# Reading moving operands and writing product columns in descending order in two stages of a two-layer decoder trunk

## The chip, the core and the metric

The kernel runs on one core of one Trainium2 chip. The metric is the device time of one execution in microseconds (us). Before the change it is 2561.69 us, the median of three runs (2560.36 to 2563.14 us). A profile of one execution gives the times of single instructions; its span, from the first to the last instruction, is 2558.4 us.

## The reference, cut to what matters

The reference is a decoder trunk on 256 tokens of width 2048, with two layers, in float32. Each layer has a token mixer (layer 0: multi-scale retention; layer 1: a short gated convolution) and a SwiGLU feed-forward of inner width 5632. Each of the four sublayers starts with an RMS norm that is scaled and shifted by columns computed from a conditioning vector.

```python
for i in range(DEPTH):
    mod = (c_act @ w_mod[i] + b_mod[i])[:, None, :]
    sh1, sc1, g1, sh2, sc2, g2 = jnp.split(mod, 6, axis=-1)
    h = rms_norm(x, norm1_g[i]) * (1.0 + sc1) + sh1
    y = retention_mixer(...) if i == 0 else short_conv_mixer(...)
    x = x + g1 * y
    h = rms_norm(x, norm2_g[i]) * (1.0 + sc2) + sh2
    x = x + g2 * swiglu(h, ffn_w_in[i], ffn_w_out[i])

def swiglu(h, w_in, w_out):
    a, b = jnp.split(h @ w_in, 2, axis=-1)
    return (jax.nn.silu(a) * b) @ w_out

def short_conv_mixer(h, w_in, conv_w, w_out):
    b_gate, c_gate, u = jnp.split(h @ w_in, 3, axis=-1)
    u = c_gate * u
    up = jnp.pad(u, ((0, 0), (CONV_WIDTH - 1, 0), (0, 0)))
    y = sum(conv_w[j] * up[:, j:j + S] for j in range(CONV_WIDTH))
    return (b_gate * y) @ w_out
```

The products that the change touches are `h @ w_in` of layer 0's feed-forward, and `h @ w_in` and `(...) @ w_out` of the convolution mixer in layer 1.

## The kernel before, in words

Every float32 factor is split into a high part (type fp32r) and a low remainder, fp32r as well. A product is then high times high, plus high times low, plus low times high. All matmuls contract over 128 partitions. The weights come from HBM in tiles of 128x2048 (`raw`, issued by `fetch`, L380), in exactly the order of use; `prepare` splits each into `hi` (ScalarE, L419) and `lo` (VectorE, L422), which lie in two rings of five places of 1024 columns. Five places ahead of the matmuls is as far as the splitting can run. VectorE also computes the conditioning columns (`modulation`, L326) between the other work.

There are two main forms of product.

- `product` (L472 and L475): a block of 128x128 weights is the stationary operand, and the activation rows are the moving one. A row tile holds the high part of 256 tokens and beside it the low part, so that one matmul of 512 columns (L472) multiplies the weights' high part by both, into a whole PSUM bank of two halves, and one of 256 columns (L475) multiplies the weights' low part by the high rows alone, into the bank's second half. Both matmuls load their stationary operand anew. One block of weights thus costs a pair of matmuls. The two halves are added when the bank is read (`summed`, or the two L714 and L715 operations of `output`).
- `thrice` (L485, L486, L487): a 128x128 piece of activations is the stationary operand, and 512 columns of weights are the moving one. The three matmuls, all of 512 columns, are high times high, high times low, low times high, into one bank.

Layer 0's feed-forward is done in two parts of 20 and 24 column tiles. `first_rows` makes the last four tiles of the first part with `normed` and `product`. All others come from `last_input`, ten times in all: `gathered` runs over eight pairs of row tiles, where five pairs go through `by_token` (eight calls of `thrice` each) and three through `sevens` (seven calls of `thrice` in place of eight, with sums of activation pieces as the stationary operands, in tiles named `sums` and `u`). That is 61 calls of `thrice` for each `last_input`, 610 in all. At the end of `last_input`, eight transposes (L1290), which wait in a list and are run inside the next group, turn the result for the second matrix. The second matrix of layer 0's feed-forward goes through `output` and `product`.

The convolution in layer 1 has 48 column tiles of its first matrix: five in `normed` (L667 to L669), 43 in `product` (43 x 16 = 688 pairs). Its second matrix has 15 tiles in `product` (240 pairs), and the last in `packed`.

Layer 1's feed-forward uses `thrice` for both matrices, with the same code as layer 0's first matrix. The retention has both forms.

The order of the matmuls is that of the program (the matrix engine's schedule is written by hand); the other engines' order is the planner's. The weights' layout in HBM follows the order of use and is checked at each `take`. The dictionary `own` holds what differs between the callers of `gathered`.

Of the kernel before, what the change touches and what calls it, by code (L numbers as in the profile page):

```python
# [44 lines left out]
FFN_TILES, FFN_SEVEN, FFN_TURNS = (20, 24), (2, 4, 6), 2  # L45
# [219 lines left out]
def trunk(ctx: ExitStack, tc: tile.TileContext, x_in, c_in, pos_in, w_mod, cols_in, gain_in, tab_in, w_all, out):  # L265
# [8 lines left out]
    def name(s):  # L274
        serial[0] += 1
        return f"{s}_{serial[0]}"

    def tmp(tag, shape=(P, S), dtype=F32, pool=work, bufs=None):
        return pool.tile(list(shape), dtype, tag=tag, name=name(tag), bufs=bufs)
# [69 lines left out]
    def paced(n):  # L349

        units[0] += n
        due = 0
        for (a, i), (b, j) in zip(plan_mod, plan_mod[1:]):
            if units[0] >= a:
                due = min(j, i + (units[0] - a) * (j - i) // (b - a))
        allowed[0] = min(allowed[0] + n * MOST, 2.0)
        while todo and n_mod - len(todo) < due and allowed[0] >= 1.0:
            allowed[0] -= 1.0
            modulation(*todo.pop())
# [71 lines left out]
    def fits():  # L431
        return prepared[0] < len(pieces) and len(ready) + 1 + (pieces[prepared[0]][1] == 6) <= PLACES

    def take(group, k, col, width=P):

        assert order.pop() == (group, k, col, width)
        i = place[0] or 0
        if i == 0:
            if place[0] == 0:
                ready.pop(0)  # L440
            while len(ready) < 1 + AHEAD * (units[0] >= first) or units[0] >= early and fits():
                n = len(ready)
                prepare()
                if len(ready) == n:
                    break
        place[0] = (i + width) % ready[0][2]
        return [t[:, i : i + width] for t in ready[0][:2]]

    def bank():
        return ps.tile([P, 2, S], F32, tag="bank", name=name("bank"))  # L450

    asides, since = [], [0]
    waiting = []

    def ticked(n):

        since[0] += n
        if asides and since[0] >= asides[0][0]:
            asides.pop(0)[1]()
            since[0] = 0  # L460

    def product(g, act, base=0, before=None, banks=None, last=True):

        fresh = not banks
        banks = banks or [bank() for _ in g.cols]
        for k in g.ks:
            if before:
                before(k)
            h = act[k - base]
            for c, pt in zip(g.cols, banks):  # L470
                hi, lo = take(g, k, c)
                nc.tensor.matmul(  # L472
                    pt, hi, h, start=fresh and k == g.ks[0], stop=False, skip_group_check=True
                )
                nc.tensor.matmul(  # L475
                    pt[:, 1, :], lo, h[:, 0, :], start=False, stop=last and k == g.ks[-1], skip_group_check=True
                )
            ticked(len(g.cols))
            paced(len(g.cols))
        return banks  # L480

    def thrice(o, x, w, first, last):

        (hi, lo), (w_hi, w_lo) = x, w
        nc.tensor.matmul(o, hi, w_hi, start=first, stop=False)  # L485
        nc.tensor.matmul(o, hi, w_lo, start=False, stop=False)  # L486
        nc.tensor.matmul(o, lo, w_hi, start=False, stop=last)  # L487
# [140 lines left out]
    def rows_at(o):  # L628
        return [
            h_all[:, o + 2 * S * j : o + 2 * S * (j + 1)].rearrange("p (a b) -> p a b", a=2) for j in range(KT)  # L630
        ]

    h = rows_at(EARLIER)
# [88 lines left out]
    with ExitStack() as inner:  # L722
# [64 lines left out]
        with tc.tile_pool(name="start", bufs=1) as sp:  # L787
# [59 lines left out]
            with tc.manual_schedule(engines={mybir.EngineType.DVE, mybir.EngineType.Activation}):  # L847
# [10 lines left out]
                part = rm.tile([P, P], F32, tag="mid17", name="part")  # L858
# [24 lines left out]
                sums = bank()[:, 0, :]  # L883
# [52 lines left out]
                def before(k):  # L936
                    if k:
                        lows[k] = row(k)
# [210 lines left out]
        h = rows_at(0)  # L1149
# [9 lines left out]
        s = b()  # L1159
        nc.vector.tensor_tensor(m, s, g1, op=ALU.mult)  # L1160

    own = {}

    def at(v, c):
        return v[:, c * DV : (c + 1) * DV]

# [134 lines left out]
    def first_rows(firsts, pairs, layer, norm, turns=()):  # L1301

        pending, done = [], 0
        for i, g in enumerate(firsts):
            pending += [sums(g)] if i else normed(acc, layer, norm, g)
            while len(pending) >= 2:
                both = half_bank().rearrange("p (a b) -> p a b", a=2)
                g1, m = both[:, 0, :], both[:, 1, :]
                silu_times(*pending[:2], g1, m)
                pending = pending[2:]  # L1310
                split(pairs[done // 2][:, done % 2], m)
                done += 1
            for turn_of in turns[4 * (i - 1) : 4 * i] if i else ():
                turn_of()

    def paired(pool, n):

        return [pool.tile([P, 2, 2, S], F32R, tag=f"mid{i}", name=name("mid")) for i in range(n // 2)]

    with tc.tile_pool(name="ffn", bufs=1) as fpool:  # L1320
        h = rows_at(EARLIER)
        own.update(pool=fpool, sums={}, turns=FFN_TURNS)
        first_mid = paired(fpool, max(FFN_TILES))[: FFN_TILES[0] // 2]
        differences[0] = fpool.tile([P, 2 * DV], F32, tag="differences", name="differences")
        own["extra"] = [fpool.tile([P, DV], F32, tag=f"extra{i}", name=f"extra{i}") for i in range(2)]
        for part in range(2):
            n = FFN_TILES[part] // 2
            mid = paired(fpool, FFN_TILES[part]) if part else first_mid
            if not part:
                first_rows(FFN_FIRSTS, mid[-2:], 0, 1)  # L1330
                made_in_sums(FFN_SEVEN, [
                    fpool.tile([P, 2, P], F32R, tag=f"sums{i}", name=f"sums{i}") for i in range(6)
                ] + [tmp("u", (P, 2, P), F32R, bufs=3) for _ in range(3)])
            for i, groups in enumerate(FFN_IN[part]):
                last_input(groups, mid[2 * i : 2 * i + 2], [None, None])
            act = {k + part * FFN_TILES[0]: mid[k // 2][:, k % 2] for k in range(2 * n)}
            acc = output(
                FFN_OUT[part], act, (0, GT2), part == 1, (lambda j: scaled_only(1, 0, j)) if part else None, base=0
            )
        h = rows_at(0)  # L1340

    mixing = ctx.enter_context(ExitStack())
# [4 lines left out]
    for i, g in enumerate(CONV_IN):  # L1347
        pending += [sums(g)] if i else normed(acc, 1, 0, g)
        while len(pending) >= 3:
# [3 lines left out]
            b, c, u = pb(tmp("bsum", pool=mpool, bufs=2)), pc(), pu()  # L1353
# [13 lines left out]


    mixing.close()
    mpool = ctx.enter_context(tc.tile_pool(name="last", bufs=1))  # L1370
    dram = ctx.enter_context(tc.tile_pool(name="dram", bufs=1, space=bass.MemoryType.DRAM))

    mpool.tile([P, 120], F32, tag="apart", name="apart")
    h = rows_at(EARLIER)
# [34 lines left out]
    turns = [lambda t=t, c=c: turn(t, c) for c in range(4) for t in range(2)]  # L1409
# [149 lines left out]
```

## Time and profile before

| what | value |
|---|---|
| median of three runs | 2561.69 us (2560.36 to 2563.14) |
| profiled execution, first to last instruction | 2558.4 us |
| TensorE matmuls (PE) | 2539.3 us busy, 13237 instructions |
| TensorE weight loads (PEld) | 2181.4 us busy |
| VectorE (DVE) | 2354.7 us busy |
| ScalarE (ACT) | 1351.2 us busy |
| read from HBM | 685.11 MB, 269 GB/s over the span |

The profiled execution's own time is its span, 2558.4 us; the median of the runs lies 3.3 us above it, which is taken as what lies around the span. Matmuls are pipelined, and the end of each is modelled: a 512-column matmul is shown as 390 ns long while the next starts 227 ns after it. What counts for the time is the distance from one start to the next, called pitch below.

### The profile page before, as it was taken

To read this page: it belongs to the slowest core of one execution; us is meant where nothing else is said; L and a number is where in the kernel's file an instruction comes from. 1 tells how busy PE (TensorE), PEld (TensorE's weight loads), DVE (VectorE), ACT (ScalarE), POOL (GpSimd) and SP (SyncE) were. 2 spreads that over 40 slices of the span, in tenths; PEclk is the share of its full clock that TensorE was granted. 3 is DMA by queue.
4 is the path that set the end of the run, shared out by engine and by line. 5 is a ranking of instruction groups with operands and counts; after the bars stand their busy time and mean duration, and the time that the engine had idled before them with its cause. 6 is when DMAs were issued, how large, how long until landed. Compare 5 with 4: busy or idle time off the path is not lost.

```text
span 2558.4 us, 34761 instructions
## 1 busy us (share of the span) xinstructions
PE 2539.3 (99%) x13237; PEld 2181.4 (85%) x13237; DVE 2354.7 (92%) x2968; ACT 1351.2 (53%) x1799; POOL 179.3 (7%) x234
## 2 busy tenths in 40 slices
PE   8999999999999999999999999999999999999998
PEld 7898888888889888888888898888998888888886
DVE  7989999898899999889999899888989999999998
ACT  5544543454456554345555454445566555555554
POOL 0000121011110001000000012000000000000001
PEclk9999999999999999999999999999999999999999
DMA  9987888879875667866667879888846465555653
GB/s 399 396 329 264 319 317 340 333 287 331 325 281 213 237 234 293 336 249 228 216 228 299 328 270 344 314 306 309 323 158 215 180 230 214 181 214 183 228 183 146
DMA packets 96695, 689.47 MB, mean 269 GB/s; under 512 B 10744, under 2 KB 12168, under 8 KB 13456
## 3 DMA queue, kind: packets, MB, share of 16 engines
q1 hardware_dynamic: 96528, 687.25, 72.2%
q8 instruction: 103, 1.69, 0.3%
q14 instruction: 64, 0.52, 0.1%
HBM read 685.11 MB, written 2.11 MB: 269 GB/s over the span
## 4 chain that ended last, share of the span: by engine, by line
PE 94%; DVE 3%; DMA 1%; ACT 1%; issue 1%; POOL 0%; SPq 0%; ACTq 0%; POOLq 0%; DVEq 0%
PE bank L472 22%; PE bank L487 17%; PE bank L485 17%; PE bank L486 17%; PE bank L475 11%; DVE lo L422 1%; PE bank L667 1%; PE bank L669 1%; PE bank L668 1%; PE bank L536 1%; PE bank L535 1%; PE bank L534 1%; DVE raw L798 1%; DMA raw<-w_all 1%; PE bank L1290 1%; PE bank L1067 1%
## 5 line engine op out<-in xcount | busy, mean ns | idle before, releaser
L419 ACT CAST hi<-raw 128x1024 fp32r<-128x1024 f32 (+1 forms) x984 | 991.1, 1019 | 936.7 <-PE bank L487 325.1
L422 DVE TENSOR_TENSOR lo<-raw,hi 128x1024 fp32r<-128x1024 f32 (+1 forms) x984 | 1143.3, 1179 | 125.6 <-ACT hi L419 116.7
L485 PE MATMUL bank<-hi,h 128*128 128x512 f32 x1540 | 602.9, 391 | 0.0
L487 PE MATMUL bank<-hi,h 128*128 128x512 f32 x1540 | 601.2, 390 | 0.0
L486 PE MATMUL bank<-lo,h 128*128 128x512 f32 x1540 | 601.1, 390 | 0.0
L326 DVE SCALAR_TENSOR_TENSOR raw<-raw,cb 128x2048 f32<-128x2048 f32 x160 | 365.4, 2285 | 8.2 <-DMA raw<-w_mod 8.0
L472 PE MATMUL bank<-h,hi 128*128 128x512 f32 x1012 | 352.8, 392 | 0.0
L487 PEld LDWEIGHTS bank<-hi,h 128*128 128x128 f32 x1540 | 289.4, 188 | 61.0
L485 PEld LDWEIGHTS bank<-hi,h 128*128 128x128 f32 x1540 | 289.6, 188 | 58.1
L486 PEld LDWEIGHTS bank<-lo,h 128*128 128x128 f32 x1540 | 289.7, 188 | 57.5
L472 PE MATMUL bank<-mid,hi 128*128 128x512 f32 x920 | 319.4, 391 | 0.0
L475 PE MATMUL bank<-h,lo 128*128 128x256 f32 x1012 | 285.0, 282 | 0.0
L475 PE MATMUL bank<-mid,lo 128*128 128x256 f32 x920 | 259.7, 282 | 0.0
L472 PEld LDWEIGHTS bank<-h,hi 128*128 128x128 f32 x1012 | 190.1, 188 | 40.3
L472 PEld LDWEIGHTS bank<-mid,hi 128*128 128x128 f32 x920 | 172.9, 188 | 35.6
L475 PEld LDWEIGHTS bank<-h,lo 128*128 128x128 f32 x1012 | 191.6, 189 | 0.5
L475 PEld LDWEIGHTS bank<-mid,lo 128*128 128x128 f32 x920 | 174.3, 189 | 0.1
L472 PE MATMUL bank<-rm,hi 128*128 128x512 f32 x496 | 172.5, 391 | 0.0
L475 PE MATMUL bank<-rm,lo 128*128 128x256 f32 x496 | 140.0, 282 | 0.0
L487 PE MATMUL bank<-hi,mid 128*128 128x512 f32 x284 | 110.9, 391 | 0.0
L485 PE MATMUL bank<-hi,mid 128*128 128x512 f32 x284 | 110.9, 391 | 0.0
L486 PE MATMUL bank<-lo,mid 128*128 128x512 f32 x284 | 110.7, 390 | 0.0
(300 smaller groups left out, 3344.2 us busy)
## 6 DMA issues: line engine op xcount, KB each, us to landing
raw<-w_all SPq DMA_DIRECT2D x456, 1024.0 KB, 5.0
raw<-w_mod SPq DMA_DIRECT2D x192, 1024.0 KB, 6.1
x<-x_in SPq DMA_DIRECT2D x4, 512.0 KB, 5.3
out<-xt SPq DMA_DIRECT2D x4, 512.0 KB, 3.0
decay<-tab_in SPq DMA_DIRECT2D x8, 128.0 KB, 4.9
x<-gate_row SPq DMA_DIRECT2D x2, 512.0 KB, 4.6
last_gain<-gain_in SPq DMA_DIRECT2D x1, 1024.0 KB
cols<-cols_in SPq DMA_DIRECT2D x1, 152.0 KB, 8.2
```

What stands on the lines that cost most here:

```text
L326: nc.vector.scalar_tensor_tensor(raw, raw, 1.0, cb, op0=ALU.mult, op1=ALU.mult, accum_out=total)
L419: nc.scalar.copy(hi[:, o], raw[:, o])
L422: nc.vector.tensor_tensor(lo, raw, hi.bitcast(F32), op=ALU.subtract)
L472: nc.tensor.matmul(pt, hi, h, start=fresh and k == g.ks[0], stop=False, skip_group_check=True)
L475: nc.tensor.matmul(pt[:, 1, :], lo, h[:, 0, :], start=False, stop=last and k == g.ks[-1], skip_group_check=True)
L485: nc.tensor.matmul(o, hi, w_hi, start=first, stop=False)
L486: nc.tensor.matmul(o, hi, w_lo, start=False, stop=False)
L487: nc.tensor.matmul(o, lo, w_hi, start=False, stop=last)
L534: nc.tensor.matmul(pt, hi, h[:, 0, :], start=first, stop=False, skip_group_check=True)
L535: nc.tensor.matmul(pt, hi, h[:, 1, :], start=False, stop=False, skip_group_check=True)
L536: nc.tensor.matmul(pt, lo, h[:, 0, :], start=False, stop=last, skip_group_check=True)
L667: nc.tensor.matmul(pt, hi, high, start=k == 0, stop=False, skip_group_check=True)
```

## The change: direction of columns

Two switches are added, both off at first. With `downward`, `thrice` gives the matmul its moving operand (512 columns of weights) and its output (a PSUM bank) with the columns in descending order: step -1 in place of +1, from the last column to the first. With `rows_downward`, `product` does the same with the moving row tile (512 columns, or the 256 of its high half) and the bank. Each product lands in the same place as before, since operand and output are turned together. `downward` is on from the beginning of layer 0's feed-forward to its end, where only the first matrix uses `thrice`; `rows_downward` is on from there to the end of the convolution. The number and order of instructions, the addresses of all tiles, the transfers and the waits stay as they are.

```diff
+    own = {}
...
             for c, pt in zip(g.cols, banks):
                 hi, lo = take(g, k, c)
+                both, rows, end, high = pt, h, pt[:, 1, :], h[:, 0, :]
+                if own.get("rows_downward"):
+                    both, rows = [v.rearrange("p a b -> p (a b)")[:, ::-1] for v in (pt, h)]
+                    end, high = end[:, ::-1], high[:, ::-1]
                 nc.tensor.matmul(
-                    pt, hi, h, start=fresh and k == g.ks[0], stop=False, skip_group_check=True
+                    both, hi, rows, start=fresh and k == g.ks[0], stop=False, skip_group_check=True
                 )
                 nc.tensor.matmul(
-                    pt[:, 1, :], lo, h[:, 0, :], start=False, stop=last and k == g.ks[-1], skip_group_check=True
+                    end, lo, high, start=False, stop=last and k == g.ks[-1], skip_group_check=True
                 )
...
     def thrice(o, x, w, first, last):
 
         (hi, lo), (w_hi, w_lo) = x, w
+        if own.get("downward"):
+            o, w_hi, w_lo = [v[:, ::-1] for v in (o, w_hi, w_lo)]
         nc.tensor.matmul(o, hi, w_hi, start=first, stop=False)
...
-    own = {}
...
         h = rows_at(EARLIER)
-        own.update(pool=fpool, sums={}, turns=FFN_TURNS)
+        own.update(pool=fpool, sums={}, turns=FFN_TURNS, downward=True)
...
                 FFN_OUT[part], act, (0, GT2), part == 1, (lambda j: scaled_only(1, 0, j)) if part else None, base=0
             )
+            own.update(downward=not part, rows_downward=bool(part))
         h = rows_at(0)
...
     mixing.close()
+    own["rows_downward"] = False
```

## The prediction

> **What bounds the kernel now.** I read the page's busy times first, then the granted clock and the chain of work that ended last, then stretches of time, one for each stage, and last the starts of single matmuls.
>
> ```profile
> span 2558.4 us, 34761 instructions
> ...
> PE 2539.3 (99%) x13237; PEld 2181.4 (85%) x13237; DVE 2354.7 (92%) x2968; ACT 1351.2 (53%) x1799; POOL 179.3 (7%) x234
> ...
> PEclk9999999999999999999999999999999999999999
> ...
> PE 94%; DVE 3%; DMA 1%; ACT 1%; issue 1%; POOL 0%; SPq 0%; ACTq 0%; POOLq 0%; DVEq 0%
> PE bank L472 22%; PE bank L487 17%; PE bank L485 17%; PE bank L486 17%; PE bank L475 11%; DVE lo L422 1%; PE bank L667 1%; PE bank L669 1%; PE bank L668 1%; PE bank L536 1%; PE bank L535 1%; PE bank L534 1%; DVE raw L798 1%; DMA raw<-w_all 1%; PE bank L1290 1%; PE bank L1067 1%
> ```
>
> The chain is matmuls, 94% of it, and the five lines that the change turns (L472, L475, L485 to L487) hold 84%. The clock is at its full grant throughout, so it has nothing to give or to lose but by a fall. The stretches below are layer 0's first feed-forward matrix (first and second row), the convolution's two matrices (third and fourth) and, for comparison, layer 1's feed-forward, which uses the same three matmuls and isn't touched.
>
> ```profile
> 818.40:988.00 169.60, 169.60 (x758) 140.00 (x757) 163.47 (x204) 97.79 (x118) 14.93 (x10) 1.00 0.62 227
> 1099.90:1354.70 254.80, 254.80 (x1140) 210.43 (x1139) 239.92 (x266) 143.42 (x159) 6.64 (x6) 1.00 0.62 226
> 1518.80:1760.00 241.20, 241.20 (x1394) 214.31 (x1393) 215.69 (x290) 118.64 (x175) 29.14 (x38) 1.00 0.85 316
> 1760.00:1840.50 80.50, 80.50 (x466) 71.49 (x466) 75.88 (x108) 41.45 (x59) 4.01 (x9) 1.00 0.82 307
> 1896.40:2548.50 652.10, 652.10 (x2915) 540.03 (x2913) 619.27 (x767) 378.06 (x458) 8.70 (x8) 1.00 0.55 195
> ```
>
> The columns are PE, PEld, DVE, ACT, POOL, then clock, DMA share and GB/s. PE is busy for the whole of each stretch. Nothing that it needs is late: ScalarE, which splits the weights, waits for PE to free a place, and not the other way round (the waits between 815 and 1840 us):
>
> ```profile
> ACT hi L419 <- PE bank L472: 231.6, 162, 4.4
> ACT hi L419 <- PE bank L487: 107.4, 121, 2.7
> ```
>
> So the time in these stages is the number of matmuls times their pitch, from one start to the next, and the change can act on that pitch alone.
>
> **The pitch, taken apart.** Two undisturbed stretches, the first and last rows of each: 96 matmuls of 512 columns in layer 1 (every third shown by its line L485, 33 rows), and 51 pairs of 512 and 256 columns in the convolution (52 rows of L472).
>
> ```profile
> 2239.68 0.39 PE L485 MATMUL bank<-hi,h 128*128 128x512 f32 x1
> ...
> 2261.44 0.39 PE L485 MATMUL bank<-hi,h 128*128 128x512 f32 x1
> ```
>
> ```profile
> 1599.31 0.39 PE L472 MATMUL bank<-h,hi 128*128 128x512 f32 x1
> ...
> 1616.99 0.39 PE L472 MATMUL bank<-h,hi 128*128 128x512 f32 x1
> ```
>
> 21.76 us / 96 = 226.7 ns for a matmul of 512 columns, and 17.68 us / 51 = 346.7 ns for a pair. If a column costs c and each matmul, with its weight load, costs f besides, then 512c + f = 226.7 and 768c + 2f = 346.7, so c = 0.417 ns and f = 13.3 ns. All that a direction could touch is c (a column read and written), f, and what comes on top of both.
>
> Something does come on top. The next rows are 17 steps in layer 0 where the stationary operand is mostly a tile of sums, and 12 pairs in layer 1's `first_rows`:
>
> ```profile
> 1131.36 0.39 PE L485 MATMUL bank<-hi,sums 128*128 128x512 f32 x1
> ...
> 1135.30 0.39 PE L487 MATMUL bank<-hi,sums 128*128 128x512 f32 x1
> ```
>
> ```profile
> 1891.81 0.40 PE L472 MATMUL bank<-h,hi 128*128 128x512 f32 x1
> ...
> 1896.05 0.40 PE L472 MATMUL bank<-h,hi 128*128 128x512 f32 x1
> ```
>
> 3.94 us / 17 = 231.8 ns, and 4.24 us / 12 = 353.3 ns: the same shapes at the same clock, 5.1 ns and 6.6 ns dearer. The weight load of the next matmul runs beside the streaming of this one, and the two reads must disturb each other more in some relative positions than in others. That is the only effect in the trace by which an order of reading could matter at full speed.
>
> **The change part by part.** No instruction, transfer, wait, queue entry or address is added, removed or moved; ScalarE, VectorE, GpSimd and the DMA queue do what they did. Two groups of matmuls change direction. Their number:
>
> ```profile
> 818.40:988.00 169.60, 95.58 (x244) 45.80 (x244) 1.00 0.62 227
> 1099.90:1354.70 254.80, 143.39 (x366) 68.72 (x366) 1.00 0.62 226
> 1896.40:2548.50 652.10, 369.21 (x944) 177.22 (x944) 1.00 0.55 195
> ```
>
> ```profile
> 1518.80:1840.50 321.70, 321.61 (x928) 174.30 (x928) 1.00 0.85 314
> ```
>
> The first are L485 by stretch, with L486 and L487 as often; the second is L472 in the convolution, with L475 as often. So 610 x 3 = 1830 matmuls in the feed-forward and 928 pairs.
>
> *Column rate.* Turned columns at the same c cost nothing. The trace has no descending operand; from below c cannot fall by any row (no shape streams faster than 0.417 ns), from above the dearest 512-column row of the kernel bounds it: the plain float32 matmuls, below, at 592 ns shown against 390, 202 ns more, or 0.39 ns for each column. I take no change, since ascending fp32r operands of all tiles, wherever they lie, show the one c.
>
> ```profile
> L518 PE MATMUL bank<-raw,u 128*128 128x512 f32 x24 | 11.3, 592 | 0.0
> ```
>
> *What lies above the floor in the feed-forward.* Both stretches last 424.4 us for 610 triples. 610 x 680.0 ns (three times 226.7) is 414.8 us, so 9.6 us are left. The transposes lie in it, 64 in the two stretches and 80 in layer 1's, in groups of eight:
>
> ```profile
> 818.40:988.00 169.60, 3.10 (x24) 2.80 (x24) 1.00 0.62 227
> 1099.90:1354.70 254.80, 5.18 (x40) 4.67 (x40) 1.00 0.62 226
> 1896.40:2548.50 652.10, 10.36 (x80) 9.34 (x80) 1.00 0.55 195
> ```
>
> ```profile
> 871.10 1.04 PE L1290 MATMUL bank<-tab,extra 128*128 128x128 f32 x8
> 871.89 0.48 PE L485 MATMUL bank<-hi,u 128*128 128x512 f32 x1
> 872.20 0.40 PE L486 MATMUL bank<-lo,u 128*128 128x512 f32 x1
> ```
>
> A group takes 0.79 us from its start to the next matmul, and that matmul is 0.08 us late to hand over (0.31 us pitch against 0.23), 0.87 us in all. Eight groups: 7.0 us. So 2.6 us, or 4.3 ns for each triple, is disturbance above the floor. In layer 1: 652.1 - 944 x 0.680 - 10 x 0.87 = 1.5 us, 1.6 ns for each triple. A turned stream meets the weight loads in another order; from below it removes all 2.6 us, from above it puts all matmuls at 231.8 ns, 1830 x 5.1 ns = 9.4 us in place of 2.6, so +6.8 us. I take the value of layer 1, the nearest row of the same code: 610 x (1.6 - 4.3) ns = -1.6 us.
>
> *The convolution.* 321.7 us / 928 = 346.7 ns: it stands on the floor already, so nothing above it is there to remove. From above, all pairs at 353.3 ns: +6.1 us. I take 0.
>
> The sum: -1.6 + 0 = -1.6 us, on the profiled 2558.4 us and so on the median, which lies 3.3 us above it: 2561.7 - 1.6 = **2560.1 us**. What hides the zeros: were c to rise by 1%, it would be paid in full, (1830 x 512 + 928 x 768) columns x 0.417 ns x 1% = 6.9 us, for PE has no idle time to cover it.
>
> [...]
>
> **The rivals.**
>
> *The 13.3 ns are themselves the meeting of two ascending reads, and opposite directions part them.* For it: f appears with each weight load, and the amount above it (5.1 and 6.6 ns) is of the same kind, so f may be the smallest such meeting and not a fixed cost. Against: it's the same 226.7 and 346.7 in stretches whose tiles lie far apart, as a fixed cost of changing the weights would be. There are 1830 + 1856 = 3686 turned matmuls: 49.0 us of f, 24.3 in the feed-forward and 24.7 in the convolution. VectorE limits the first: it is busy 163.5 + 239.9 = 403.4 us of 424.4, so no more than 21 us can be had there before it sets the pace; in the convolution it has 291.6 of 321.7 and the transfers 0.85, enough. So 0 to -45.7 us; half of f, since no row says more, gives -24.5 us and 2537.2 us.
>
> *Opposite reads meet in a worse way* (the other side). Every turned matmul falls into the dear pattern shown above: +6.8 us and +6.1 us, 2574.6 us. For it: the convolution and most triples sit in the cheapest pattern there is, so a shift can only raise them. Of the 12.9 us, 5.1 are reached, and the kernel is measurably slower, once 0.4 of the turned matmuls fall into that pattern.
>
> *A step of -1 isn't streamed at a column per 0.417 ns.* At twice c: 1.65 million columns x 0.417 ns = +687 us, 3249 us. For it: no row shows such an operand. Against: the banks and rows stay dense, only the order turns. Any loss of c beyond 0.7% makes the kernel slower. [...]
>
> *The switches don't act where they say* (a tile made twice, an operand turned and not its output) would change results, and not the time: 2561.7 us, counted with the forecast.
>
> **How the numbers follow.** A measurement of this kernel can tell about 0.2%, 5.1 us, from no change. Forecast (floor kept, a small change of disturbances): 0.42. Rival one, the parted reads: 0.34, nearly all of it beyond 5 us. Rival two, the worse meeting: 0.16, nearly all beyond 5 us. Rival three: 0.08. Hence faster 0.34, same 0.42, slower 0.24. The range reaches down to 2530 us, two thirds of f, which leaves out some 0.08 of rival one, and up to 2582 us, rival two and the smallest losses of rival three; what is left out above is the rest of that, some 0.06. As cases of both signs hold over half of the chance, the forecast's own range is 2557 to 2566 us.
>
> **What would show each step.** If c and f are kept, the convolution's 928 pairs take 321 to 323 us and undisturbed triples 680 ns. Under rival one the pairs fall below 340 ns and VectorE's share of the feed-forward's stretches rises toward 100%. Under rival two the pairs stand at 350 to 354 ns. Under rival three the shown length of L485 in layer 0 departs from 390 ns by far more than 10 ns, while layer 1's stays. Other stages must keep their times within a microsecond or so; if they don't, the reason isn't in the direction. I am wrong if the convolution's pair leaves 346 to 348 ns.

## The result, and the profile after

The changed kernel takes 2576.28 us (median of four runs, 2574.25 to 2579.50) against 2561.20 us for the kernel before beside it (four runs, 2560.36 to 2563.14). The ratio is 1.0059 with a 95% interval of 1.0045 to 1.0073: slower, by 15.1 us. The forecast was 2560.1 us.

The page of the changed kernel, from its head, its busy times, its clock and its chain (the product is now L477 and L480, `thrice` is L492 to L494):

```profile
span 2577.7 us, 34756 instructions
...
PE 2557.4 (99%) x13237; PEld 2182.8 (85%) x13237; DVE 2354.9 (91%) x2968; ACT 1351.2 (52%) x1799; POOL 176.8 (7%) x234
...
PEclk9999999999999999999999999999999999999999
...
PE 93%; DVE 4%; issue 2%; ACT 1%; DMA 1%; POOL 0%; POOLq 0%; ACTq 0%; DVEq 0%
```

The same 13237 matmuls are 18.1 us longer busy. VectorE, ScalarE and the weight loads have nearly their old times. The five fewer instructions in the head are waits for semaphores (13 fewer on VectorE, 8 more on the matrix engine), so the waits didn't stay quite as they were; a run below that has the same ones, `output_alone`, is no slower than before. The stretches that answer to those shown of before (PE, PEld, DVE, ACT, POOL, clock, DMA share, GB/s):

```profile
821.10:994.50 173.40, 173.40 (x758) 140.09 (x757) 163.67 (x203) 97.49 (x118) 13.94 (x10) 1.00 0.61 223
1106.40:1366.90 260.50, 260.50 (x1140) 210.50 (x1139) 240.20 (x266) 143.09 (x159) 6.66 (x6) 1.00 0.61 222
1534.20:1859.90 325.70, 325.70 (x1858) 283.63 (x1857) 291.73 (x397) 159.39 (x232) 32.25 (x47) 1.00 0.83 310
1915.80:2568.10 652.30, 652.30 (x2915) 539.58 (x2913) 619.24 (x769) 378.10 (x459) 8.88 (x8) 1.00 0.54 195
```

PE still has no idle time in them, so their length is again number times pitch. To measure a stage to 0.01 us, take the start of its first matmul and of the first one behind it. These are the timeline's rows of before for the two parts of layer 0's feed-forward and for the convolution:

```profile
818.45 0.39 PE L485 MATMUL bank<-hi,h 128*128 128x512 f32 x1
...
988.11 0.40 PE L472 MATMUL bank<-mid,hi 128*128 128x512 f32 x1
...
1099.94 0.39 PE L485 MATMUL bank<-hi,h 128*128 128x512 f32 x1
...
1354.83 0.40 PE L472 MATMUL bank<-mid,hi 128*128 128x512 f32 x1
...
1518.89 0.39 PE L472 MATMUL bank<-h,hi 128*128 128x512 f32 x1
...
1840.59 0.28 PE L534 MATMUL bank<-mid,hi 128*128 128x256 f32 x1
```

And of after, with starts of single matmuls between them: those from which the prediction took its pitches (1138.61 and 1142.58: 17 steps with `sums`; 1615.64 and 1633.55: 51 pairs; 2259.07 and 2280.82: 96 matmuls of layer 1), and from 1120.41 to 1138.61 a stretch of 26 triples:

```profile
821.13 0.40 PE L492 MATMUL bank<-hi,h 128*128 128x512 f32 x1
...
994.58 0.40 PE L477 MATMUL bank<-mid,hi 128*128 128x512 f32 x1
...
1106.41 0.40 PE L492 MATMUL bank<-hi,h 128*128 128x512 f32 x1
...
1120.41 0.40 PE L492 MATMUL bank<-hi,h 128*128 128x512 f32 x1
...
1138.61 0.40 PE L492 MATMUL bank<-hi,sums 128*128 128x512 f32 x1
...
1142.58 0.40 PE L494 MATMUL bank<-hi,sums 128*128 128x512 f32 x1
...
1367.01 0.40 PE L477 MATMUL bank<-mid,hi 128*128 128x512 f32 x1
...
1534.18 0.40 PE L477 MATMUL bank<-h,hi 128*128 128x512 f32 x1
...
1615.64 0.40 PE L477 MATMUL bank<-h,hi 128*128 128x512 f32 x1
...
1633.55 0.40 PE L477 MATMUL bank<-h,hi 128*128 128x512 f32 x1
...
1860.01 0.28 PE L541 MATMUL bank<-mid,hi 128*128 128x256 f32 x1
...
2259.07 0.39 PE L492 MATMUL bank<-hi,h 128*128 128x512 f32 x1
...
2280.82 0.39 PE L492 MATMUL bank<-hi,h 128*128 128x512 f32 x1
```

| stage | before, us | after, us | more |
|---|---|---|---|
| feed-forward, first matrix, part one | 988.11 - 818.45 = 169.66 | 994.58 - 821.13 = 173.45 | 3.8 |
| second matrix, part one (not turned) | 1099.94 - 988.11 = 111.83 | 1106.41 - 994.58 = 111.83 | 0.0 |
| first matrix, part two | 1354.83 - 1099.94 = 254.89 | 1367.01 - 1106.41 = 260.60 | 5.7 |
| convolution, both matrices | 1840.59 - 1518.89 = 321.70 | 1860.01 - 1534.18 = 325.83 | 4.1 |

The turned stages lose 13.6 us and the stage between them nothing. The pitch says how: a pair costs 17.91 us / 51 = 351.2 ns in place of 346.7; a 512-column matmul of the feed-forward 3.97 us / 17 = 233.5 ns, where the cheapest were 226.7 and those of the stretch with `sums` 231.8 in the mean. A level somewhat above that mean is now the one of all triples, whatever their tiles: 18.20 us / 26 = 700.0 ns, 233.3 for each matmul. Layer 1's feed-forward, not turned, keeps 21.75 us / 96 = 226.6 ns. The shown length moved with it; this group of 520, from the feed-forward's two parts and the second matrix between them, stood at 390 ns before:

```profile
L492 PE MATMUL bank<-hi,h 128*128 128x512 f32 x520 | 206.6, 397 | 0.0
```

The profiled span is 19.3 us longer, not 13.6. Of the rest, 2.7 us lie ahead of 774 us, before anything is turned, and 3.1 us in the `normed` stage ahead of the convolution, which isn't turned either. There the matrix engine waits once, in the waits of PE between 1490 and 1540 us, and 1.7 us behind that wait its granted clock falls to half for 3.4 us (the clock is the third number from the end of the second row):

```profile
PE bank L579 <- ACT acc L565: 1.4, 1, 1.4
...
1508.20:1511.60 3.40, 3.40 (x19) 3.40 (x18) 2.79 (x2) 1.05 (x1) 0.29 (x1) 0.51 0.93 337
```

The matmuls of this stage start 214 ns apart there, in place of 119. Wait and clock are worth about 1.6 and 1.5 of the 3.1 us. The page's row of tenths can't show so short a fall. Ahead of 774 us there is another, to 0.50 from 108.8 to 112.2 us. In another execution that turns the same reads (the second experiment) these two stages differ from before by 2.4 and 0.2 us, and in those below that leave the tiles in their places by 0.0 to 2.1 and by 0.0 us. So these stages vary from one execution to the next, and the 13.6 us are what the change costs. (What lies around the span is 1.8 us here, 2579.50 against 2577.7, not the 3.3 us that were taken for it before the change.)

### The profile page after: what moved, and what is told of

Same layout as the page of the kernel before. It is cut to its first block, busy times and chain, and to the rows that moved or that the text cites. A ratio compares the mean times of both kernels' runs of the same rounds, so it can differ in the third digit from the quotient of the medians.

```text
span 2577.7 us, 34756 instructions
## 1 busy us (share of the span) xinstructions
PE 2557.4 (99%) x13237; PEld 2182.8 (85%) x13237; DVE 2354.9 (91%) x2968; ACT 1351.2 (52%) x1799; POOL 176.8 (7%) x234
## 4 chain that ended last, share of the span: by engine, by line
PE 93%; DVE 4%; issue 2%; ACT 1%; DMA 1%; POOL 0%; POOLq 0%; ACTq 0%; DVEq 0%
PE bank L477 21%; PE bank L492 17%; PE bank L494 17%; PE bank L493 17%; PE bank L480 11%; DVE lo L422 2%; PE bank L674 1%; PE bank L676 1%; PE bank L675 1%; PE bank L542 1%; PE bank L543 1%; PE bank L541 1%; PE bank L1295 1%; PE bank L1074 1%; DMA raw<-w_mod 1%
## 5 line engine op out<-in xcount | busy, mean ns | idle before, releaser
L492 PE MATMUL bank<-hi,h 128*128 128x512 f32 x1540 | 606.3, 394 | 0.0
L494 PE MATMUL bank<-hi,h 128*128 128x512 f32 x1540 | 604.1, 392 | 0.0
L477 PE MATMUL bank<-h,hi 128*128 128x512 f32 x1012 | 355.9, 397 | 0.0
L494 PEld LDWEIGHTS bank<-hi,h 128*128 128x128 f32 x1540 | 289.4, 188 | 64.3
L492 PEld LDWEIGHTS bank<-hi,h 128*128 128x128 f32 x1540 | 289.7, 188 | 61.3
L477 PE MATMUL bank<-mid,hi 128*128 128x512 f32 x920 | 320.4, 392 | 0.0
L480 PE MATMUL bank<-h,lo 128*128 128x256 f32 x1012 | 284.7, 281 | 0.0
L480 PE MATMUL bank<-mid,lo 128*128 128x256 f32 x920 | 259.4, 282 | 0.0
L477 PEld LDWEIGHTS bank<-h,hi 128*128 128x128 f32 x1012 | 190.1, 188 | 45.0
L477 PEld LDWEIGHTS bank<-mid,hi 128*128 128x128 f32 x920 | 172.7, 188 | 37.6
L480 PEld LDWEIGHTS bank<-h,lo 128*128 128x128 f32 x1012 | 190.5, 188 | 0.5
L480 PEld LDWEIGHTS bank<-mid,lo 128*128 128x128 f32 x920 | 173.6, 189 | 0.1
L477 PE MATMUL bank<-rm,hi 128*128 128x512 f32 x496 | 172.5, 390 | 0.0
L480 PE MATMUL bank<-rm,lo 128*128 128x256 f32 x496 | 139.8, 282 | 0.0
L494 PE MATMUL bank<-hi,mid 128*128 128x512 f32 x284 | 110.8, 390 | 0.0
L492 PE MATMUL bank<-hi,mid 128*128 128x512 f32 x284 | 110.7, 390 | 0.0
```

The lines of the kernel that those rows point to most:

```text
L477: nc.tensor.matmul(both, hi, rows, start=fresh and k == g.ks[0], stop=False, skip_group_check=True)
L480: nc.tensor.matmul(end, lo, high, start=False, stop=last and k == g.ks[-1], skip_group_check=True)
```

## The experiments

Each kernel was run once with a profile, and `sums_moved` in five rounds. A single time has no interval, so verdicts rest on stages: those that an edit leaves alone, like the second matrix of the feed-forward, repeat within 0.02 us, while whole runs of the kernel before spread from 2560.07 to 2565.52 us. Stages are measured as in the table above. "Feed-forward" below means its first matrix, both parts together, 9.5 us dearer under the change; the convolution is 4.1 us dearer. Short diffs are against the kernel after, unless another is named.

| run | time, us | feed-forward, us more | mean triple, ns | convolution, us more | mean pair, ns |
|---|---|---|---|---|---|
| before | 2561.20 | 0 | 686 | 0 | 346.7 |
| after | 2576.28 | 9.5 | 701 | 4.1 | 351.1 |
| output_alone | 2560.26 | 0.0 | 686 | 0.0 | 346.7 |
| operand_alone | 2576.40 | 9.5 | 701 | 4.1 | 351.1 |
| first_of_group | 2571.01 | 4.2 | 692 | 6.2 | 353.3 |
| others_of_group | 2570.66 | 9.4 | 701 | 0.4 | 347.1 |
| one_column_up | 2567.09 | 6.2 | 696 | 0.0 | 346.7 |
| one_column_down | 2575.55 | 9.5 | 701 | 4.1 | 351.1 |
| ring_moved (+32 B) | 2607.10 | 9.5 | 701 | 6.2 | 353.3 |
| ring_16 | 2605.57 | 10.0 | 702 | 6.2 | 353.3 |
| ring_48 | 2590.49 | 9.5 | 701 | 6.2 | 353.3 |
| blocks_down | 2575.83 | 9.5 | 701 | 6.2 | 353.3 |
| inside_down | 2680.37 | 70.4 | 801 | 49.5 | 400.0 |
| sums_moved | 2559.95 | -0.4 | 685 | 0.0 | 346.7 |

The means take in the matmuls beside the transposes. The theory at the start was the prediction's second rival, that the moving operand's read, once turned, meets the weight load's reads worse. Against it stood the output: PSUM columns written downwards could cost as much by themselves.

### Output or operand

Only the columns in PSUM descend, the reads ascend:

```diff
-                    both, rows = [v.rearrange("p a b -> p (a b)")[:, ::-1] for v in (pt, h)]
-                    end, high = end[:, ::-1], high[:, ::-1]
+                    both = pt.rearrange("p a b -> p (a b)")[:, ::-1]
+                    end = end[:, ::-1]
+                    rows = h.rearrange("p a b -> p (a b)")
...
-            o, w_hi, w_lo = [v[:, ::-1] for v in (o, w_hi, w_lo)]
+            o = o[:, ::-1]
```

> Only the PSUM side of the turned matmuls descends; their moving operands ascend as before the change. Each product thus lands mirrored in its bank, so the values that follow are others than the reference's; the instructions are the same ones. Theory 'reads' (the rise comes from the order in which the moving operand is read beside the weight load): the feed-forward's triples stay at 680 to 686 ns and the convolution's pairs at 346.7 ns, the two stages at 424.5 and 321.7 us. Rival 'writes' (descending PSUM columns cost it): 700 ns and 351.1 ns as with the whole change, 434.0 and 325.8 us.

2560.26 us, beside 2560.30 for the kernel before. No stage moved by 0.1 us. The same 51 pairs of the convolution, from its timeline:

```profile
1599.40 0.39 PE L478 MATMUL bank<-h,hi 128*128 128x512 f32 x1
...
1617.08 0.39 PE L478 MATMUL bank<-h,hi 128*128 128x512 f32 x1
```

17.68 us, to the hundredth what it was. The counterpart turns the reads and leaves the output ascending:

```diff
-                    both, rows = [v.rearrange("p a b -> p (a b)")[:, ::-1] for v in (pt, h)]
-                    end, high = end[:, ::-1], high[:, ::-1]
+                    both = pt.rearrange("p a b -> p (a b)")
+                    rows = h.rearrange("p a b -> p (a b)")[:, ::-1]
+                    high = high[:, ::-1]
...
-            o, w_hi, w_lo = [v[:, ::-1] for v in (o, w_hi, w_lo)]
+            w_hi, w_lo = [v[:, ::-1] for v in (w_hi, w_lo)]
```

> Only the moving operands descend; the PSUM columns ascend as before the change, so that the products land mirrored again and the values aren't the reference's. Theory 'reads': 700 ns for a triple and 351.1 ns for a pair, 434.0 and 325.8 us, all of the rise. Rival 'writes': 680 to 686 ns and 346.7 ns, none of it. If both runs show a part, both sides cost.

2576.40 us, and the turned stages cost 9.5 and 4.1 us more, as under the whole change. The rows of 32 triples and 51 pairs, 22.40 us / 32 = 700.0 ns and 17.91 us / 51 = 351.2 ns:

```profile
1120.14 0.40 PE L493 MATMUL bank<-hi,h 128*128 128x512 f32 x1
...
1142.54 0.40 PE L493 MATMUL bank<-hi,h 128*128 128x512 f32 x1
...
1538.00 0.40 PE L478 MATMUL bank<-h,hi 128*128 128x512 f32 x1
...
1555.91 0.40 PE L478 MATMUL bank<-h,hi 128*128 128x512 f32 x1
```

This is settled: of the two things that the change turns, the reading order of the moving operand carries the whole cost, and the order of the output has no part in it.

### Which matmul of the group

If each turned matmul paid its own price, the prices of two halves would add up. First half: the first of each triple and the 512-column one of each pair are turned, the rest ascend.

```diff
-                    end, high = end[:, ::-1], high[:, ::-1]
...
-            o, w_hi, w_lo = [v[:, ::-1] for v in (o, w_hi, w_lo)]
-        nc.tensor.matmul(o, hi, w_hi, start=first, stop=False)
+            first_o, first_w = [v[:, ::-1] for v in (o, w_hi)]
+        nc.tensor.matmul(first_o, hi, first_w, start=first, stop=False)
```

> Operand and output descend together, but only in the first matmul of each triple (L492 of the changed kernel) and in the 512-column one of each pair. Theory 'each turned matmul of 512 columns pays 6.7 ns by itself': a third of the triple's rise, 680 + 6.7 = 686.7 ns on the average, and all of the pair's, 351.1 ns. Rival 'the state is handed from one matmul to the next' (what a matmul costs depends on where the streams before it stopped): values off this scale, such as 680 or 700 for the triple, and a pair other than 351.1 ns.

Its timeline, 32 triples in the feed-forward and 51 pairs in the convolution:

```profile
1115.99 0.40 PE L492 MATMUL bank<-hi,h 128*128 128x512 f32 x1
...
1138.09 0.40 PE L492 MATMUL bank<-hi,h 128*128 128x512 f32 x1
...
1530.68 0.40 PE L476 MATMUL bank<-h,hi 128*128 128x512 f32 x1
...
1548.70 0.40 PE L476 MATMUL bank<-h,hi 128*128 128x512 f32 x1
```

690.6 ns for a triple and 353.3 for a pair. The other half turns the second and third of each triple and the 256-column one of each pair:

```diff
-                    both, rows = [v.rearrange("p a b -> p (a b)")[:, ::-1] for v in (pt, h)]
...
+        first_o, first_w = o, w_hi
...
-        nc.tensor.matmul(o, hi, w_hi, start=first, stop=False)
+        nc.tensor.matmul(first_o, hi, first_w, start=first, stop=False)
```

> The complement: the second and third matmul of each triple and the 256-column one of each pair descend. Theory 'each turned matmul of 512 columns pays 6.7 ns by itself, one of 256 columns nothing': 680 + 13.3 = 693.3 ns for the triple and 346.7 ns for the pair. Rival 'the state is handed on': off this scale, and a pair that moves although its 512-column matmul ascends.

```profile
1118.37 0.39 PE L492 MATMUL bank<-hi,h 128*128 128x512 f32 x1
...
1140.77 0.39 PE L492 MATMUL bank<-hi,h 128*128 128x512 f32 x1
...
1535.92 0.39 PE L476 MATMUL bank<-h,hi 128*128 128x512 f32 x1
...
1553.60 0.39 PE L476 MATMUL bank<-h,hi 128*128 128x512 f32 x1
```

700.0 ns and 346.7 ns. The halves give 4.2 + 9.4 = 13.6 us in the feed-forward, where the whole gives 9.5, and 6.2 + 0.4 = 6.6 us in the convolution, where it gives 4.1. A price for each turned matmul by itself falls. In the convolution the 512-column reads carry nearly all of it, and turning the 256-column ones as well takes back 2 us. What a matmul costs depends on its neighbours: a pair with its 512-column read turned takes 353.3 ns beside an ascending 256-column read and 351.2 beside a descending one.

### A weight load that reads one address

If the price is the meeting of two walks, the stream's and the load's, it should go when the load doesn't walk. Here the stationary operand is one column, repeated 128 times, first with the moving operand ascending, then descending:

```diff
-                    both, rows = [v.rearrange("p a b -> p (a b)")[:, ::-1] for v in (pt, h)]
-                    end, high = end[:, ::-1], high[:, ::-1]
+                    hi, lo = [v[:, 0:1].to_broadcast([P, P]) for v in (hi, lo)]
...
-            o, w_hi, w_lo = [v[:, ::-1] for v in (o, w_hi, w_lo)]
+            hi, lo = [v[:, 0:1].to_broadcast([P, P]) for v in (hi, lo)]
```

> As before the change (all ascending), but in the two stages every weight load reads its first column 128 times (a step of 0) in place of 128 columns, so that all rows of a product are alike and the values aren't the reference's; the number and shape of the instructions stay. Theory 'the moving read meets the weight load's read': with one address for the whole load the meetings end or become even, and the triple falls below 680 ns and the pair below 346.7 ns, by up to the 13.3 ns that a matmul costs beside its columns (640 and 320 ns would be all of it). Rival 'the 13.3 ns are the change of weights itself': 680 and 346.7 ns stay, and only what lies above them in the feed-forward (2.6 us) may go.

```profile
1117.09 0.39 PE L491 MATMUL bank<-hi,h 128*128 128x512 f32 x1
...
1139.33 0.39 PE L491 MATMUL bank<-hi,h 128*128 128x512 f32 x1
...
1532.98 0.39 PE L476 MATMUL bank<-h,hi 128*128 128x512 f32 x1
...
1550.65 0.40 PE L476 MATMUL bank<-h,hi 128*128 128x512 f32 x1
```

> The same with the change (moving operands and outputs descending). Theory 'the moving read meets the weight load's read': the triple and the pair come to the values of the ascending run with one column, within a nanosecond, so that the direction no longer matters. Rival 'a descending read is slower by itself': 20 ns for each triple and 4.4 ns for each pair stay between the two runs, 9.5 and 4.1 us in the stages.

The descending run's 51 pairs:

```profile
1537.45 0.40 PE L478 MATMUL bank<-h,hi 128*128 128x512 f32 x1
...
1555.36 0.40 PE L478 MATMUL bank<-h,hi 128*128 128x512 f32 x1
```

A triple takes 695.0 ns with ascending reads, more than the 687 of the same 32 triples before, and 700.0 with descending ones; a pair 346.5 ns ascending (17.67 us / 51) and 351.2 ns descending. So the 13.3 ns above the columns don't vanish when the load's addresses stop walking, and in the convolution the change costs its 4.1 us all the same. The theory in its simple form, two walks that collide, falls. The rival, a descending read that is slower by itself, expected 20 and 4.4 ns between the two runs: the pair has about its 4.4, the triple only 5. That the load matters somehow is shown by the feed-forward's 10 ns in the mean; in which way stays open.

### The place of the weights, modulo 64 bytes

If the relative place of the two reads matters, shifting one must move the pitch of reads that still ascend. The traces hold no addresses, so what is known here is by how much the rings move, not where they lie. That places 64 B apart are alike was the author's assumption; no run shows it. Three kernels keep the change and move the rings `hi` and `lo` by 32, 16 and 48 B. The rings are the stationary operand in `product` and the moving one in `thrice`, in every stage, so the stages that aren't turned test it.

```diff
+    wpool.tile([P, 8], F32, tag="ahead", name="ahead")
     split_weights = [
         wpool.tile([P, PLACES * HALF], F32R, tag=tag, name=tag) for tag in ("hi", "lo")
     ]
+    wpool.tile([P, 8], F32, tag="behind", name="behind")
```

> The changed kernel with the two rings of split weights 32 bytes further on, and everything else at the same place within 64 bytes as before. Nothing is left out. Theory 'the moving read meets the weight load's read, place by place': the pitch of stages that ascend changes with the distance of the two operands, so layer 1's feed-forward leaves its 652.4 us by several us (5 ns for each matmul would be 14 us), and the descending stages may leave 700 ns and 351.1 ns. Rival 'only the direction counts': 652.4 us, 700 ns and 351.1 ns stay.

2607.10 us: the stages that aren't turned became dear. The same 96 matmuls of layer 1, and 51 pairs of the second feed-forward matrix in layer 0:

```profile
1390.11 0.40 PE L479 MATMUL bank<-mid,hi 128*128 128x512 f32 x1
...
1408.13 0.40 PE L479 MATMUL bank<-mid,hi 128*128 128x512 f32 x1
...
2278.91 0.40 PE L494 MATMUL bank<-hi,h 128*128 128x512 f32 x1
...
2301.32 0.40 PE L494 MATMUL bank<-hi,h 128*128 128x512 f32 x1
```

22.41 us / 96 = 233.4 ns, and 18.02 us / 51 = 353.3 ns: ascending reads at a shift of 32 B cost what descending reads cost, within 2.2 ns. Layer 1's feed-forward loses 17.1 us, the second matrix 2.1 and 2.4 us, all that lies ahead of layer 0's feed-forward 10 us. In the second matrix the moving rows stay where they were within 64 B and only the weights that are loaded move against them, so the place of the loaded weights changes the pitch of the stream, 346.7 to 353.3 ns. The next two moved the rings by 16 B (4 elements) and 48 B (12 elements):

```diff
-        wpool.tile([P, PLACES * HALF], F32R, tag=tag, name=tag) for tag in ("hi", "lo")
+        wpool.tile([P, PLACES * HALF + 16], F32R, tag=tag, name=tag)[:, 4 : 4 + PLACES * HALF]
+        for tag in ("hi", "lo")
```

> The changed kernel with both rings of split weights 16 bytes further on within 64 bytes, the rest where it was. Nothing is left out. Theory 'a descending read has a good distance too, at another offset': the triples of layer 0 fall from 700 towards 680 ns here or with 48 bytes; layer 1's, which ascend, leave 682.5 ns. Rival 'descending never does': layer 0 stays at 695 to 705 ns at both offsets, while layer 1's ascending ones go to about 700 ns, as they did with 32 bytes.

> The same with 48 bytes. The two theories expect what they expect of 16 bytes; if a good distance exists at a step of 16 bytes, it's at one of 16 and 48, as 0 and 32 bytes showed 700 to 701 ns for descending reads.

The pitches of those 96 and 51 matmuls, and for the turned stages the means of the table above:

| rings moved by | layer 1's triple (ascending) | second matrix's pair (ascending) | feed-forward's triple (descending) | convolution's pair (descending) |
|---|---|---|---|---|
| 0 B | 680 ns | 346.7 ns | 701 ns | 351.1 ns |
| 16 B | 698 ns | 353.3 ns | 702 ns | 353.3 ns |
| 32 B | 700 ns | 353.3 ns | 701 ns | 353.3 ns |
| 48 B | 691 ns | 346.7 ns | 701 ns | 353.3 ns |

From the profile of the kernel with 48 B, the same pairs of the second matrix stay at the floor (17.68 us / 51):

```profile
1382.06 0.39 PE L478 MATMUL bank<-mid,hi 128*128 128x512 f32 x1
...
1399.74 0.39 PE L478 MATMUL bank<-mid,hi 128*128 128x512 f32 x1
```

Ascending reads have cheap places and dear ones. Descending reads were dear at all four. This makes the result readable: 226.7 and 346.7 ns aren't a fixed cost of a matmul and its weight load but a good position, and the change gives it up for a level that is dear wherever it was tried. Whether a descending read has a good position elsewhere or simply costs more by itself, these runs don't separate.

### Inside 64 bytes, or over the whole tile

Two kernels split the descent: blocks of 16 columns (64 B) in descending order with the columns in each ascending, and the reverse.

```diff
-                    both, rows = [v.rearrange("p a b -> p (a b)")[:, ::-1] for v in (pt, h)]
+                    both, rows = [
+                        v.rearrange("p a (b c) -> p (a b) c", c=16)[:, ::-1, :] for v in (pt, h)
+                    ]
...
-            o, w_hi, w_lo = [v[:, ::-1] for v in (o, w_hi, w_lo)]
+            o, w_hi, w_lo = [v.rearrange("p (b c) -> p b c", c=16)[:, ::-1, :] for v in (o, w_hi, w_lo)]
```

> The complement: blocks of 16 columns descend, the columns within each ascend. Nothing is left out. Theory 'near': 680 to 686 ns and 346.7 ns, as before the change. Rival 'far': 700 ns and 351.1 ns. A third outcome, above 701 ns or below 680 ns in either run, would say that a two-dimensional operand has a cost of its own.

Blocks downwards: 701 ns a triple, and in the convolution 18.01 us for the same 51 pairs, 353.1 ns:

```profile
1610.40 0.40 PE L479 MATMUL bank<-h,hi 128*128 128x512 f32 x1
...
1628.41 0.40 PE L479 MATMUL bank<-h,hi 128*128 128x512 f32 x1
```

So it is enough to lose the good position that the walk over the tile descends; the order inside 64 B needn't. No run shows what an operand in blocks costs by itself. The triple's pitch is that of the plain descent, the pair's is 2.2 ns above it. The reverse has `[:, :, ::-1]` in place of `[:, ::-1, :]`:

> The same matmuls are turned as in the change, but only inside blocks of 16 columns (64 bytes): the blocks ascend, the columns within each descend, in operand and output alike. Nothing is left out. Theory 'near' (what counts is the order within 64 bytes, where 32 bytes of offset already moved the pitch): 700 ns for a triple and 351.1 ns for a pair, as with the whole change. Rival 'far' (what counts is how the two reads drift towards or away from each other over whole tiles): 680 to 686 ns and 346.7 ns, as before.

```profile
1682.49 0.43 PE L479 MATMUL bank<-h,hi 128*128 128x512 f32 x1
...
1702.89 0.43 PE L479 MATMUL bank<-h,hi 128*128 128x512 f32 x1
```

20.40 us / 51 = 400.0 ns for a pair and 800 for a triple, far above every other run: the third outcome, which neither theory had. A matmul of 512 columns takes 800 / 3 = 266.7 ns, 40 more than the floor. That is 0.521 ns for each column, and so is the pair's 400.0 ns for 768 columns: nothing is left that each matmul would cost besides. The 13.3 ns of the floor don't come on top of this slower stream, which again speaks against a fixed cost of changing the weights. This pattern has a cost of its own, so it can't say whether the order inside a block matters for the position.

### The sums

The prediction read the dear matmuls with `sums` as a matter of place. This moves the `sums` tiles by 32 B in the kernel before (diff against it):

```diff
+        fpool.tile([P, 8], F32, tag="beside_sums", name="beside_sums")
```

> The kernel before, all ascending, with the tiles of sums of layer 0's feed-forward (and the tiles u512) 32 bytes further on, where the other stationary operands already stand within 64 bytes. Nothing is left out. Theory 'place by place': the disturbance above the floor in layer 0's feed-forward goes the way of layer 1's, 2.6 us down to about 1 us or less, and the kernel gets 1.5 to 2.6 us faster, 2559 against 2561. Rival 'only the direction counts': no change in the stage's 424.5 us.

2559.95 us (median of 11) against 2560.49 (15): ratio 0.9998, 0.9989 to 1.0007, no change. The feed-forward gained 0.4 us of the 2.6 that lie above the floor. The sum hides that the place does count. These are the pitches at the 60 triples with `sums`, as means of the starts in the two traces:

| pitch of | before, ns | `sums` moved, ns |
|---|---|---|
| the matmul ahead of the triple (the next load is a `sums` tile) | 235.2 | 227.2 |
| its first matmul | 232.2 | 234.4 |
| its second | 230.1 | 232.2 |
| its third (the next load is a plain tile) | 232.4 | 235.8 |

The matmul ahead falls to the floor, though its own operands stay in their places, and the three of the triple get dearer. Together these 240 matmuls stay 1.4 us above the floor, and the 0.4 us come from other triples. So the place of a stationary tile decides which matmul is dear, but this move doesn't bring the saving that the theory expected.

No kernel of the study is measurably faster than the one before.

## Why the prediction was wrong, and where it was right

**The frame held.** The matrix engine bounds the turned stages, its clock stays at full there (1.00 in each stretch), nothing else is late, and the time is number times pitch: 610 triples and 928 pairs carry the 13.6 us, and the second matrix between them stays within 0.02 us wherever the rings keep their place. The bounds were near, too: from above, 6.8 and 6.1 us; measured, 9.5 and 4.1. That their sum, 12.9 us, comes so close to 13.6 is in part luck, since one was 2.7 us short and the other 2.0 us too long.

**The step that failed is the choice between the bounds.** In the feed-forward the prediction took layer 1's disturbance as "the nearest row of the same code", 610 x (1.6 - 4.3) ns = -1.6 us, and in the convolution 0, because it "stands on the floor already". Those rows belong to reads in the old order. A floor was read as something that a turn can't disturb, when the sentence under rival two, that a shift from the cheapest pattern "can only raise them", was the argument to follow. Measured: every triple at 700 ns, 610 x 20.0 = 12.2 us above the floor, of which 2.6 were there before, so 9.6 (9.5 by the stages); every pair at 351.1 ns, 928 x 4.4 = 4.1 us.

**The upper bound of the feed-forward was 2.7 us short** because it priced the dear matmul at 231.8 ns from the stretch with `sums`. That stretch mixes matmuls, 225 to 239 ns from one start to the next, and the turned ones stand at 233.3: 1830 x 1.5 ns = 2.7 us. The convolution came out below its bound: with the weights in their old place, turning both matmuls of a pair costs less than turning the larger one alone (351.1 against 353.3 ns); why stays open.

**Rival two was right** in sign and nearly in size, 2574.6 us against 2576.28: the turned matmuls fall near the dear level that the trace had shown elsewhere (233.3 ns against 231.8, a pair 351.1 against 353.3). Its mechanism, a worse meeting of the two reads, was an inference and isn't shown: the price stays when the load reads one address (700.0 and 351.2 ns). Its test, pairs of 350 to 354 ns, and the prediction's own condition of being wrong, a pair outside 346 to 348, both came in. It had a chance of 0.16, less than half of rival one's.

**Rival one was wrong**: no stretch became faster in any turned form. The 13.3 ns were taken for a meeting of two ascending reads that opposite reads would part. A load that reads one address doesn't remove them (346.5 ns a pair and 695.0 a triple with the moving operand ascending), and under a slower stream (0.521 ns for each column) they don't come on top.

**The column rate** can't be separated as the prediction did it. Its two equations with the new pitches, 512c + f = 233.3 and 768c + 2f = 351.1, give c = 0.451 ns and f = 2.3 ns; with the pitches of ascending reads at a shift of 32 B (233.4 and 353.3) they give 0.443 and 6.4. Once the floor is lost, a pair's extra is neither in proportion to columns nor to matmuls, so c and f of the floor are a description of that position and no parts of the cost. A rate of its own for descending reads isn't needed, since ascending ones reach the same pitch, but it isn't excluded either. Rival three, a step that isn't streamed, didn't occur: the shown length went from 390 to 397 ns.

**The place of the load, and the PSUM side.** That direction could matter at all rested on the inference that the read of the next weights and that of the moving operand disturb each other. What the runs show is the effect of a place: with the moving rows in place within 64 B, 32 B of offset of the loaded weights take the second matrix's pair from 346.7 to 353.3 ns. How much of the change's 13.6 us comes about in that way isn't shown. The PSUM side has no part in it: descending columns of the bank alone cost 0.0 us over 3686 matmuls (2560.26 us beside 2560.30).

**The other stages** were to stay "within a microsecond or so". In the profiled execution two didn't, by 2.7 and 3.1 us; a wait and falls of the clock stand there, and other executions of the same reads don't have all of them.

What stays open is the inside of it: what in the read of the weights or of the stream makes a position good, and whether a descending read costs something by itself. For a cost of its own speak the descending triples, at 700 to 702 ns with the rings at four places and at 700.0 with a load of one address. For a matter of place speaks that ascending reads reach the same level, and that a descending pair moves between 351.1 and 353.3 ns with the place of the weights. Placing the stationary operand in descending order as well, so that both reads turn, wasn't tried, nor was an offset finer than 16 B.

## What to carry to other kernels

A stage that ran matmul after matmul on the lowest pitch seen (226.7 ns for 512 columns, 346.7 for a pair) never gained from a new reading order or offset of its operands here; it kept its pitch or lost it. Price such a move by the dearest pitch that the same shape shows elsewhere in the trace. Read moving operands upwards (the other order cost 13.6 us here), and look at the pitch again after every change of the tiles' layout: 32 B of padding in front of the weights cost 31 us here (2607.10 against 2576.28). Turning the output in PSUM cost nothing in these two forms of product (2560.26 us beside 2560.30), if a layout needs it.

## What the runs showed of the hardware that was not expected

- A 512-column fp32r matmul with its own weight load has a pitch of 226.7 ns at the best place of its operands that was tried and 230.3 to 233.4 at others, at a mean granted clock of 0.998 to 0.999 in each of these executions, with all reads ascending (16, 32 and 48 B in layer 1's feed-forward).
- A descending moving operand stands at 233 to 234 ns at every place tried (0, 16, 32, 48 B), and at 353.3 ns for a pair of 512 and 256 columns, or 351.1 with the weights in their old place.
- The place of the loaded weights moves the pitch of the stream beside the load: 346.7 to 353.3 ns for a pair at 32 B, and 235.2 to 227.2 ns for the matmul ahead of a `sums` tile.
- Turning some matmuls of a group can cost more than turning all of them (353.3 against 351.1 ns), and turning two of three as much as all three (701 ns).
- A moving operand of ascending blocks of 16 columns, descending inside, costs 40 ns more for 512 columns, 0.521 ns for each column and nothing for each matmul; descending blocks, ascending inside, cost as much as a plain descent for a triple (701 ns) and 2.2 ns more for a pair (353.3 against 351.1).
- Loading 128 times the same column isn't a cheaper weight load for the stream beside it: 695 to 696 ns for a triple, against 686 to 687.
